# Linear attention on one core: first K and V issued before the tile part closes, programs of three engines moved to aligned blocks and four engines held to the end

## The chip, the cores and the metric

The kernel runs on one core of a Trainium2 chip. The metric is the device time of one execution in microseconds (us). Before the change it is 124.9 us, the median of three runs (124.57 to 125.02).

## The reference

Q, K and V are float32 of shape 8 x 12 x 512 x 64 (batch, heads, sequence, dimension), from a normal draw. With `Qf = max(0, Q)` and `Kf = max(0, K)`, each of the 96 heads computes

- `KV = Kf^T V` (64 x 64) and `Ksum = sum over the sequence of Kf` (64),
- `out = (Qf KV) / (Qf Ksum + 1e-10)`, float32.

There is no softmax, so each of Q, K and V is read once and the output is written once: 37.75 MB read and 12.58 MB written.

## The kernel before, in words

The 96 heads are cut into 12 octets of 8 heads. One octet of one tensor is 128 partitions by 2048 elements, 1 MB of float32. Everything is written for one octet and repeated 12 times. No scheduler takes part: the five engines have programs written out by hand and meet at semaphores.

- GpSimd (POOL) issues nearly all loads (`load`, L109). They cast float32 to bf16 on the way into a ring of six slots each for K, V and Q. Only Q of octet 0 (L96) goes to a slot of its own. POOL also issues the stores of octets 0 to 9 (`store`, L117). Before a load it waits until the ring slot is free again, and before a store until the octet is normed. The order is fixed: eleven rounds of K, V, Q, with stores from the eighth round on.
- SyncE (SP) issues K of octet 0 (L94) as float32 into the output buffer `o_sb[0]`, the stores of octets 10 and 11 (L117), then waits for all twelve stores (L318) and clears the kernel's semaphores (L321).
- ScalarE (ACT) issues V of octet 0 (L95) into `o_sb[1]`. Then per octet it applies relu to the transposed Q out of PSUM (L214), moves the K^T V sums out of PSUM (L219), scales a part of the next V (L208) and copies the products (L228).
- VectorE (DVE) first fills masks, zeros and an identity (L275 to L298). Then per octet: `prep` (relu and mask of K at L237, mask of V at L241), `stage` (a copy of Q, L247), `norm` (the product with the reciprocal, L259) and `denominators` (L262 to L273).
- TensorE (PE) runs `turn` in a hardware loop of 12 rounds (L189): transposes of Q (L158), K^T V (L167), the transposes back of the octet before (`back`, L148), denominators (L176), Q KV (L184). After the loop `back` runs once more. The head of the loop is at the start of an instruction block (`head_slot`).

What stands at the beginning: line 15 closes the tile framework's context at once, before any instruction of the kernel. The closing puts two rounds of an all-engine barrier behind the launch's own barrier (the profile gives them lines 16 and 334). Only behind them come L94, L95 and L96. PE waits at L188 until DVE has finished its masks (`ID` at 4); the first transposes wait for `STG` in any case, which DVE raises after that.

What stands at the end: POOL, ACT, PE and DVE run out of their programs one after the other while SP still waits for the stores.

Octets are stored from nine output buffers in turn (`NOUT`); `norm` waits for the store of nine octets before (L253).

## Time and profile before

| | us |
|---|---|
| median of three runs | 124.9 (124.57 to 125.02) |
| profiled execution, device time | 124.66 |
| its span, from the first to the last instruction | 123.4 |
| POOL busy | 27.5 (22%) |
| DVE busy | 89.3 (72%) |
| PE busy | 87.4 (71%) |
| ACT busy | 79.4 (64%) |
| HBM traffic over the span | 408 GB/s (37.75 MB read, 12.58 MB written) |

How to read it: the span counts from the first instruction that the profiler shows, and all positions below count from there. The 1.3 us between span and device time lie outside it. A load that casts moves 1 MB out of HBM and 0.5 MB into the core's memory; the GB/s of the profile count the half, so 213 GB/s in a stretch of such loads are 426 GB/s read. The chain of work that ended last is 34% DMA and 27% "issue", which is here POOL waiting for ring slots.

The trace also lists each DMA packet (queue, start, length, bytes) and each landing: a transfer of 1 MB is spread over 16 DMA engines, and each of them raises the transfer's semaphore by one when its part is in place. So for each transfer there are 16 landings. Instruction blocks that an engine fetches are packets too, on queues of their own ("instruction" in the profile): 16,384 bytes on one such queue, 8,192 on the other.

### The profile page before, as it was taken

What the parts mean: (1) busy time and instruction counts of PE and PEld (TensorE: products, weight loads), DVE (VectorE), ACT (ScalarE), POOL (GpSimd) and SP (SyncE); (2) the same over time, 40 slices, a digit from 0 to 9 for tenths busy, and PEclk for the clock granted to TensorE, in tenths of its full rate; (3) what the DMA queues carried; (4) which work ended last, traced back from release to release, by engine and by line L of the source; (5) the groups of instructions that cost most, each with busy time, mean ns of one, the idle gap of its engine ahead of it and who ended that gap; (6) DMA issues with size and microseconds to landing.
All of it is one profiled execution on the core that took longest, in us unless ns stands there. A gap on an engine that the chain in (4) does not pass through costs nothing.

```text
span 123.4 us, 3380 instructions
## 1 busy us (share of the span) xinstructions
PE 87.4 (71%) x1456; PEld 75.9 (62%) x1456; DVE 89.3 (72%) x178; ACT 79.4 (64%) x109; POOL 27.5 (22%) x50
## 2 busy tenths in 40 slices
PE   0000099998998979799897998979449939977400
PEld 0000099986886868688686877958429928947200
DVE  3737906599989899998989989897395497091600
ACT  0043063999988888898888889888539649542000
POOL 3999500050240804309101001010010001000000
PEclk9999999999999999999999999999985995996775
DMA  3999999999999999999999999999999999999994
GB/s 43 369 344 217 213 213 213 213 215 213 214 213 213 213 215 213 214 214 217 214 213 214 213 214 221 371 217 214 375 222 214 343 425 428 425 422 433 420 425 170
DMA packets 6918, 32.57 MB, mean 264 GB/s; under 512 B 768, under 2 KB 768, under 8 KB 5120
## 3 DMA queue, kind: packets, MB, share of 16 engines
q0 software_dynamic: 6336, 28.31, 92.2%
q1 hardware_dynamic: 432, 3.15, 6.6%
q10 hardware_dynamic: 144, 1.05, 2.2%
q8 instruction: 2, 0.03, 0.1%
q14 instruction: 4, 0.03, 0.1%
HBM read 37.75 MB, written 12.58 MB: 408 GB/s over the span
## 4 chain that ended last, share of the span: by engine, by line
DMA 34%; issue 27%; POOL 18%; PE 8%; DVE 5%; ACT 1%; POOLq 0%; DVEq 0%
DMA q_all<-in_Q_dram 34%; POOL k_all L109 6%; POOL q_all L109 5%; POOL v_all L109 5%; DVE o_sb L259 5%; PE ps_o L148 4%; PE ps_kv L167 2%; PE ps_q L158 1%; PE ps_o L184 1%; POOL out_dram L117 1%; ACT ot L228 1%; POOL q_all L96 1%; POOL ident L121 0%; POOL ident L119 0%; POOLq L107 0%
## 5 line engine op out<-in xcount | busy, mean ns | idle before, releaser
L259 DVE TENSOR_TENSOR o_sb<-ps_o,rec 128x1024 f32<-128x1024 f32 x24 | 28.3, 1219 | 7.0 <-PE ps_o L148 6.7
L228 ACT COPY ot<-ps_o 128x1024 f32<-128x1024 f32 x24 | 24.2, 1013 | 10.3 <-PE ps_o L184 9.2
L167 PE MATMUL ps_kv<-vo,kf 64*128 64x132 bf16 x768 | 28.6, 230 | 0.7
L148 PE MATMUL ps_o<-ident,ot 128*128 128x128 f32 x208 | 27.1, 286 | 1.1 <-ACT ot L228 1.1
L167 PEld LDWEIGHTS ps_kv<-vo,kf 64*128 64x128 bf16 x768 | 24.8, 100 | 3.8 <-DVE vo L241 2.3
L214 ACT ACTIVATE qt_sb<-ps_q 128x1024 bf16<-128x1024 bf16 x24 | 23.4, 1030 | 5.1 <-PE ps_q L158 5.1
L158 PE MATMUL ps_q<-ident,q_sb 128*128 128x128 bf16 x192 | 15.3, 243 | 15.4 <-DVE q_sb L247 15.4
L148 PEld LDWEIGHTS ps_o<-ident,ot 128*128 128x128 f32 x208 | 23.8, 146 | 2.7 <-ACT ot L228 1.4
L158 PEld LDWEIGHTS ps_q<-ident,q_sb 128*128 128x128 bf16 x192 | 13.2, 110 | 16.7 <-DVE q_sb L247 15.4
L219 ACT CAST kvd<-ps_kv 64x260 bf16<-64x260 f32 x48 | 18.0, 375 | 7.8 <-PE ps_kv L167 7.4
L184 PE MATMUL ps_o<-qt_sb,kvd 128*128 128x256 bf16 x96 | 15.0, 282 | 10.8 <-DVE o_sb L259 9.8
L237 DVE TENSOR_SCALAR kf<-k_all,mask_k 128x1024 bf16<-128x1024 bf16 x44 | 18.3, 459 | 5.6 <-PE ps_kv L167 5.4
L184 PEld LDWEIGHTS ps_o<-qt_sb,kvd 128*128 128x128 bf16 x96 | 7.7, 100 | 15.6 <-DVE o_sb L259 15.0
L241 DVE TENSOR_SCALAR vo<-v_all,mask_v 128x1024 bf16<-128x1024 bf16 x33 | 15.0, 483 | 0.9 <-DMA v_all<-in_V_dram 0.9
L109 POOL DMA_DIRECT2D k_all<-in_K_dram x11 | 8.4, 763 | 32.1 <-DVE vo L241 32.0
L117 POOL DMA_DIRECT2D out_dram<-o_sb x10 | 5.3, 533 | 40.7 <-DVE o_sb L259 40.7
L208 ACT ACTIVATE vo<-v_all,mask_v 128x1024 bf16<-128x1024 bf16 x11 | 12.7, 1155 | 0.3
L247 DVE COPY q_sb<-q_all 128x2048 bf16<-128x2048 bf16 x12 | 8.3, 694 | 5.7 <-DMA q_all<-in_Q_dram 5.7
L109 POOL DMA_DIRECT2D q_all<-in_Q_dram x11 | 8.9, 811 | 0.0
L109 POOL DMA_DIRECT2D v_all<-in_V_dram x11 | 7.6, 687 | 0.0
L176 PE MATMUL ps_q<-kvd,qt_sb 128*128 128x16 bf16 x192 | 6.9, 180 | 0.0
L176 PEld LDWEIGHTS ps_q<-kvd,qt_sb 128*128 128x128 bf16 x192 | 6.7, 96 | 0.2
(24 smaller groups left out, 27.8 us busy)
## 6 DMA issues: line engine op xcount, KB each, us to landing
out_dram<-o_sb POOLq DMA_DIRECT2D x10, 1024.0 KB, 39.8
q_all<-in_Q_dram POOLq DMA_DIRECT2D x12, 512.0 KB, 36.7
k_all<-in_K_dram POOLq DMA_DIRECT2D x11, 512.0 KB, 33.1
v_all<-in_V_dram POOLq DMA_DIRECT2D x11, 512.0 KB, 34.8
out_dram<-o_sb SPq DMA_DIRECT2D x2, 1024.0 KB, 8.4
o_sb<-in_K_dram SPq DMA_DIRECT2D x1, 1024.0 KB, 8.5
o_sb<-in_V_dram ACTq DMA_DIRECT2D x1, 1024.0 KB, 8.8
```

What stands on the lines that cost most here:

```text
L109: PL.dma_start(out=t[:, to:to + n], in_=X[o:o + n].rearrange("n p f -> p n f"), single_packet=True).then_inc(land(f"{c}{o}"), 16)
L148: t = PE.transpose(ps_o[j][:, P * v:P * v + P], ot[:, 8 * j + v].rearrange("p h c -> p (h c)"), ident32)
L158: t = PE.transpose(dst[:, u], q_sb[:, j * (U // 2) + u], ident)
L167: t = PE.matmul(ps_kv[:, half, 0:2 * (D + 2)].rearrange("p (t d) -> p t d", t=2), kf[g][rows, r].rearrange("p s d -> p (s d)"), vo[g][rows ...
L176: t = PE.matmul(ps_den[:, u], qt_sb[:, u], kvd[:, :, 0:2 * D1:2 * D1 - 1], start=True, stop=True, skip_group_check=True)
L184: t = PE.matmul(ps[:, h], kvd[:, 4 * j + h, 1:2 * D + 1], q[:, :, 4 * j + h, :], start=True, stop=True, skip_group_check=True)
L214: AC.activation(qt_sb[:, j * (U // 2):(j + 1) * (U // 2)], ps_q[j].bitcast(bf16).rearrange("p (u f) -> p u f", u=U // 2), Act.Relu)
L219: t = AC.copy(kvd[64 * c:64 * c + 64, s::2, c * D1:c * D1 + D1].rearrange("p (g t) d -> p g t d", t=2), ps_kv[64 * s:64 * s + 64, :, 0:2 * ...
L228: t = AC.copy(ot[:, :, 4 * j:4 * j + 4], ps_o[j].rearrange("p (h u c) -> p u h c", h=4, u=U))
L237: VE.tensor_scalar(kf[g][:, :, s, :], k_rows(o, g), scalar1=0.0, scalar2=mask_k[:, s:s + 1], op0=Alu.max, op1=Alu.mult)
L241: x = VE.tensor_scalar(vo[g][:, :, t, 2:D + 2], v_rows(o, g), scalar1=mask_v[:, t:t + 1], scalar2=None, op0=Alu.mult)
L259: VE.tensor_tensor(dst[:, rs], ps_o[j].rearrange("p (r d) -> p r d", d=D), rec[o % 2][:, rs].unsqueeze(2).to_broadcast([P, R, D]), op=Alu. ...
```

## The change

K and V of octet 0 are issued inside the tile part, in a critical section, before it is closed, so they stand behind the launch's barrier and ahead of the closing's two. Because the tile part now holds instructions, its closing has semaphores of its own to clear; POOL does that between the two barriers.

POOL, ACT and DVE get an alignment directive after the closing (`at_line`): the next instruction is placed at the next multiple of 128 instruction slots, and a branch skips the padding.

At the end, POOL, PE, ACT and DVE each wait for the stores (`hold`) and raise `FIN`; SP waits for `FIN` at 4 and clears. The twelve store semaphores become three single ones (octets 0 to 2, which `norm` waits for), one shared by octets 3 to 9 (`ALL`) and one shared by octets 10 and 11 (`LAST`). PE's wait for `ID` goes away.

```diff
-    tc.close()
-    tc.compile()
...
+    FETCH = 128
...
-    stored = sems(*[f"st{o}" for o in range(NO)])
+    ALL, LAST, FIN = sems("all", "last", "fin")
+    stored = [sems(f"st{o}")[0] if o + NOUT < NO else ALL if o < NO - 2 else LAST for o in range(NO)]
...
-    SP.dma_start(out=k8.rearrange("p r d -> p (r d)"), in_=Kr[0]).then_inc(land("k0"), 16)
-    AC.dma_start(out=v8.rearrange("p r d -> p (r d)"), in_=Vr[0]).then_inc(land("v0"), 16)
+    def at_line(eng):
+        eng.addr_align(FETCH, offset=0, max_nops=0)
+
+    def hold(eng):
+        eng.wait_ge(ALL, 16 * (NOUT - 2))
+        eng.wait_ge(LAST, 32)
+        eng.sem_inc(FIN, 1)
+
+    with tc.tile_critical(no_gpsimd_drain=True):
+        SP.dma_start(out=k8.rearrange("p r d -> p (r d)"), in_=Kr[0]).then_inc(land("k0"), 16)
+        AC.dma_start(out=v8.rearrange("p r d -> p (r d)"), in_=Vr[0]).then_inc(land("v0"), 16)
+
+    tc.close()
+    tc.compile()
+    for eng in (PL, AC, VE):
+        at_line(eng)
     PL.dma_start(out=q_all[:, RING], in_=Qr[0], single_packet=True).then_inc(land("q0"), 16)
...
     for i in range(done, NO - 2):
         store(PL, i)
+    hold(PL)
     for i in range(NO - 2, NO):
         store(SP, i)
...
-    PE.wait_ge(ID, 4)
     with nc.Fori(1, NO + 1, engines=bass.OrderedEngineSet([PE.engine]), head_slot={PE.engine: 0}) as i:
         turn(i)
     PE.wait_ge(OT, NO + 1)
     back(0)
     back(1)
+    hold(PE)
...
         t.then_inc(OT, 1)
+    hold(AC)
...
     norm(NO - 1)
-    for s in stored:
-        SP.wait_ge(s, 16)
+    hold(VE)
+    SP.wait_ge(FIN, 4)
```

## The prediction

> **What bounds the kernel.** I read the page's slices and DMA queues first, then the beginning by engine, then narrow windows at both ends, then the waits of SP's queue, and last the trace's packets and landings.

> ```profile
> DMA  3999999999999999999999999999999999999994
> ...
> q8 instruction: 2, 0.03, 0.1%
> q14 instruction: 4, 0.03, 0.1%
> ```

> The 16 DMA engines are full from the second slice to the last but one, so no compute engine is the bound: the time is when the transfers start, plus their length, plus what is left when the last one ends. The two queues below move instruction blocks and seem negligible; they are not, as shown further on. The beginning (start, duration, engine and line):

> ```profile
> 1.40 0.38 SPq L94 DMA_DIRECT2D o_sb<-in_K_dram  x1
> 1.40 0.39 ACTq L95 DMA_DIRECT2D o_sb<-in_V_dram  x1
> ...
> 1.93 0.67 POOL L96 DMA_DIRECT2D q_all<-in_Q_dram  x1 [1.48 <-POOLq L16]
> ```

> K and V are issued at 1.40 us. Narrow windows (columns end with DMA share and GB/s):

> ```profile
> 2.00:3.50 1.50, 0.00 (x0) 0.00 (x0) 1.12 (x2) 0.00 (x0) 1.10 (x4) 1.00 0.88 137
> 3.50:8.00 4.50, 0.00 (x0) 0.00 (x0) 2.81 (x19) 0.70 (x1) 4.50 (x9) 1.00 0.97 381
> ...
> 120.00:121.00 1.00, 0.00 (x0) 0.00 (x0) 0.00 (x0) 0.00 (x0) 0.00 (x0) 0.50 0.99 418
> 121.00:121.50 0.50, 0.00 (x0) 0.00 (x0) 0.00 (x0) 0.00 (x0) 0.00 (x0) 0.50 0.59 246
> 121.50:122.00 0.50, 0.00 (x0) 0.00 (x0) 0.00 (x0) 0.00 (x0) 0.00 (x0) 0.50 0.20 82
> 122.00:122.50 0.50, 0.00 (x0) 0.00 (x0) 0.00 (x0) 0.00 (x0) 0.00 (x0) 0.50 0.20 82
> ```

> The transfers ramp up for 1.5 us and then run full. At the end most of the 16 engines are done by 121.5, but a share of 0.20, three engines of 16, goes on to 122.5. The waits of SP's queue (total us, times, longest) hold the two barriers' price:

> ```profile
> SPq L334 <- PEq L334: 0.7, 1, 0.7
> SPq L16 <- PEq L16: 0.5, 2, 0.3
> ```

> SP leaves the launch's barrier at 0.66 and the closing's second at 1.32.

> **The stragglers at the end.** In the trace's landings, the last store's 16 parts have their median at 121.76, but four come 0.91, 0.93, 1.28 and 1.37 later, and SP's final wait ends with the latest. The packets say why. Six instruction blocks were fetched while data flowed: 16,384 bytes at 11.50 (took 0.94) and 114.34 (0.97), 8,192 at 32.75, 49.66, 97.46 and 105.55 (0.31 each). From the first one on, one landing of sixteen is late by 1.2 in every transfer, where the three before had at most 0.21. A fetch runs on one DMA engine, and since the queues never empty, that engine never catches up. Whose blocks these are I infer from the instruction counts. The 16 KB ones are PE's: it enters its loop at 7.78 and leaves it at 110.36, with its program running into the next block some 12 slots later. The fetch follows such an entry by 3.7 (7.78 to 11.50). DVE executes 123 instructions between 32.75 and 97.46, about one block, so those are its two. The one at 105.55 comes 3.2 after POOL's last issue ends (102.31): POOL runs on past its program. 49.66 is ACT's.

> **The change part by part.**

> *K and V earlier.* Behind the launch's barrier (SP free at 0.68) stand now a no-operation, a wait for its own count and the issue. The rows between SP's instructions in the barriers are 0.06 apart, so the issue comes at 0.86 to 0.92, ACT's about the same. Against 1.40 that is 0.48 to 0.54. The ramp (first packet 1.01 after the issue) moves with it. Since everything behind it is a full queue, each later transfer moves by it too: **-0.5**. Bounds: 0 (if the ramp waits for something else) and -0.74 (the whole of 0.66 to 1.40).

> *The closing later.* SP and ACT must finish their issues (0.38, 0.39) and report before the closing's first barrier: 0.9 + 0.39, four steps of 0.06 and a barrier of 0.33 put its release at about 1.76. POOL's clearing stands between the barriers (SP's own at the end lasts 0.145 and is the nearest row; I take 0.1 with its drain), then the second barrier at 0.33: POOL is free at 2.15 where it was at 1.29, **0.85 later**, and so are DVE, ACT and PE. Is that covered? DVE's fills end at 7.22 and it then waits 2.75 for K; moved to 8.1 they still end before or at K's landing. ACT's table load (7.30 to 8.58) moves to 9.5 and V is not there before 8. PE starts at 15.4 on DVE's copy. For these three the cost is 0, or up to 0.3 of compute that the full queue hides anyway.

> *POOL's own issue* is the one that can hurt. Q of octet 0 is issued at 1.93 to 2.59, and its first packet runs at 6.31. Until then DMA lives on K and V alone: 16 packets per engine, the first two within 1.45 (2.41 to 3.86), 14 more at 0.306, so alone they last until 2.41 + 1.45 + 4.28 = 8.14, with the change 7.6. Q's first packet moves to 6.31 + 0.85 = 7.16. Margin 0.45: cost 0. POOL's many issues at 0.53 each stay far ahead of DMA (a load lands 33 to 37 after its issue).

> *The alignment.* Three branches over padding, and a new block each. The nearest rows are PE's jump into its aligned loop, 7.35 to 7.78, so at most 0.43 per engine, and a gap of 0.06 between plain instructions. I take 0.1: with POOL at 7.26, still inside the margin. In return ACT's program (about 111 instructions behind the directive) and POOL's (about 55) lie in one block of 128, so the fetches at 49.66 and 105.55 go, and DVE's two become one, near 68. The blocks behind are now asked for at 2.2, while K and V flow, at 0.31 each on their engines. PE enters its loop at about 2.7 instead of 7.78, so its first 16 KB also fall into K's and V's time: the engine is late by 1.0 from there on, as before from 11.5.

> *PE's last fetch*, at 114.34, is the one that decides. The loop is 244 slots (120 products of two instructions each, and four more) of a block of 256, so the 32 slots behind it cross the block's end exactly as before, whether PE is held afterwards or not. I expect the 16 KB again, hence a part 1.1 to 1.3 late. Of the 1.37 now, 0.1 to 0.26 was there before (the landings before 114 show it) and may go: **-0.1**, bounds +0.3 (another early block on the same DMA engine) and -1.2 (no such fetch).

> *The hold.* Last landing, a wait of 0.02 to 0.05 on four engines, one hop to SP (0.03 from a release to its receiver), the clear: **+0.05**; 0 to +0.15. SP's six waits were in line already, so nothing is won. PE's wait for `ID` covered nothing: its first transposes wait for DVE until 15.4.

> Sum: -0.5 - 0.1 + 0.05 = **-0.55** on the profiled 124.66, that is 124.1. That execution lies 0.24 under the median of the runs, to which I carry the gain: 124.9 - 0.55 = 124.35, said as **124.4**. About 0.5%, 0.62 us, is what a measurement of this kernel can tell from no change, so the forecast ends just inside "no difference".

> [...]

> **Rivals.**

> 1. *The stragglers go.* If PE, held, does not fetch at 114, and its early block falls into the ramp, where DMA moves 137 instead of 381 GB/s and has room, the last landing comes 0.2 to 0.8 behind the median instead of 1.37: 0.6 to 1.2 more, 123.1 to 123.8. For it: early requests meet empty queues. Against: PE's crossing is the same, and the request comes 0.8 after K's first packet.

> 2. *DMA runs dry after K and V* (slower). If POOL finds its new block not yet there, it waits for the fetch: 3.2 to 3.7 by the two rows above. Q's first packet then comes at about 10.7, K and V are out at 7.6, and DMA idles 3.0: -0.5 + 3.0 = +2.5, 127.4. It decides from 0.45 of stall on, and the kernel is slower by over 0.5% from 1.6 on; a partial stall gives 125.5 to 126.5. For it: POOL's first issue already comes 0.63 after its release, unexplained. Against: the target is the very next block, and DVE, ACT and POOL show no stall at their crossings now.
> [...]

> 3. *Nothing reaches the end.* The start is won, but two early blocks fall on one DMA engine, or PE's last one on an engine already late by 0.31: -0.5 + 0.3 + 0.1, 124.8.

> **Chances.** Forecast 0.55 (own range 124.0 to 124.9; of it 0.19 below 124.28, which is faster by over 0.5%, 0.36 within). Stragglers go 0.15 (faster). DMA dry 0.22 (0.20 slower, 0.02 within). Nothing reaches the end 0.08 (within). Faster 0.34, within 0.46, slower 0.20. The range takes rival 1 nearly whole and the partial stalls: 123.2 to 125.7.

> **What would show it.** K's issue at 0.86 to 0.92 and its first packet at 1.9; POOL's first issue at 2.7 to 2.9; no gap in DMA at 7 to 8; no instruction packet between 10 and 110 but DVE's near 68; one 16 KB packet near 114 and a last landing 1.1 to 1.3 behind its median. I am wrong if that packet is missing, if POOL's first issue comes after 4, or if the time outside the span (1.3) grows because four held engines now end after the stores.

## The result, and the profile after

The changed kernel takes 127.98 us, the median of six runs (127.82 to 129.65), against 124.86 of the kernel before (124.45 to 125.02) on the same chip. The ratio is 1.0288 with a 95% interval of 1.0254 to 1.0322: slower by 3.1 us, where 124.4, just inside a difference of 0.5%, was forecast. The profiled execution took 127.87, its span is 126.17.

The page of the changed kernel, by slices of 3.2 us:

```profile
span 126.2 us, 3391 instructions
...
POOL 0029997023050431707400101010010000000000
...
DMA  4958999999999999999999999999999999999993
GB/s 75 410 192 156 165 212 213 213 213 216 212 213 214 216 212 213 214 213 213 213 214 212 213 213 217 352 238 217 332 260 213 306 426 423 429 431 421 423 434 156
```

POOL does nothing in the first two slices but fill constants, and DMA, which before the change was full from the second slice on, has a hole from the third slice to the fifth (192, 156 and 165 GB/s, where the row shows some 213 for loads that cast). From there on the row reads as before. The beginning, by the changed kernel's timeline (start, duration, engine and line; "idle before" in brackets):

```profile
0.91 0.39 ACTq L105 DMA_DIRECT2D o_sb<-in_V_dram  x1
0.95 0.38 SPq L104 DMA_DIRECT2D o_sb<-in_K_dram  x1
...
8.32 0.67 POOL L111 DMA_DIRECT2D q_all<-in_Q_dram  x1 [7.87 <-issue]
8.98 0.22 POOL L134 MEMSET ident<- 128x128 bf16 x1
```

K and V go out 0.45 and 0.49 earlier, as wanted. But POOL's first issue, Q of octet 0, comes at 8.32 instead of 1.93, with no semaphore that held it ("issue": the engine waited for nothing that the profile shows). The trace has POOL's branch over the padding at 2.36. The same in windows (DMA share and GB/s at the end of the row), one of the kernel before:

```profile
8.00:11.00 3.00, 0.00 (x0) 0.00 (x0) 1.03 (x2) 1.41 (x2) 3.00 (x7) 1.00 1.08 264
```

and three of the changed kernel:

```profile
3.50:8.00 4.50, 0.00 (x0) 0.00 (x0) 3.11 (x16) 0.00 (x0) 0.00 (x0) 1.00 0.96 386
8.00:11.00 3.00, 0.00 (x0) 0.00 (x0) 0.90 (x4) 0.22 (x1) 2.27 (x6) 1.00 0.42 71
11.00:14.00 3.00, 0.00 (x0) 0.00 (x0) 2.96 (x5) 2.21 (x2) 3.00 (x5) 1.00 0.95 173
```

K and V are in place at 8.2 to 8.4 (median of their 16 landings), Q's first packet runs at 9.69, and for three microseconds DMA moves about a quarter of what it moved there before (71 GB/s against 264).

Where the 3.21 us between the two profiled executions are: K of octet 1 lands at 16.45 against 13.56, **2.89** later, although K and V of octet 0 began 0.48 earlier. From then on the shift stays: Q of octet 11 lands 2.82 later (medians 99.98 and 97.16), the span is 2.81 longer. The other **0.4** lies outside the span, 1.70 against 1.30. The tail did not change: the last landing comes 1.33 behind its median, before 1.37.

### The profile page after: what moved, and what is told of

Read it like the earlier page. It is cut to its first block, busy times and chain, and to the rows that moved or that the text cites. A ratio compares the mean times of both kernels' runs of the same rounds, so it can differ in the third digit from the quotient of the medians.

```text
span 126.2 us, 3391 instructions
## 1 busy us (share of the span) xinstructions
PE 86.5 (69%) x1456; PEld 75.3 (60%) x1456; DVE 89.1 (71%) x178; ACT 79.4 (63%) x109; POOL 28.2 (22%) x50
## 4 chain that ended last, share of the span: by engine, by line
DMA 33%; issue 27%; POOL 18%; PE 6%; DVE 6%; ACT 1%; POOLq 0%; DVEq 0%
DMA q_all<-in_Q_dram 33%; POOL q_all L124 6%; POOL k_all L124 6%; DVE o_sb L277 6%; POOL v_all L124 5%; PE ps_kv L183 2%; PE ps_o L164 2%; PE ps_q L174 1%; PE ps_o L200 1%; POOL out_dram L132 1%; ACT ot L244 1%; POOL q_all L111 1%; POOL ident L136 0%; POOL ident L134 0%; DVEq L276 0%
## 5 line engine op out<-in xcount | busy, mean ns | idle before, releaser
L183 PE MATMUL ps_kv<-vo,kf 64*128 64x132 bf16 x768 | 29.7, 235 | 0.7
L183 PEld LDWEIGHTS ps_kv<-vo,kf 64*128 64x128 bf16 x768 | 25.9, 103 | 3.8 <-DVE vo L259 2.3
L164 PE MATMUL ps_o<-ident,ot 128*128 128x128 f32 x208 | 25.8, 278 | 1.1 <-ACT ot L244 1.1
L164 PEld LDWEIGHTS ps_o<-ident,ot 128*128 128x128 f32 x208 | 22.7, 142 | 2.8 <-ACT ot L244 1.4
L124 POOL DMA_DIRECT2D k_all<-in_K_dram x11 | 7.3, 663 | 27.3 <-DVE vo L259 27.1
L124 POOL DMA_DIRECT2D q_all<-in_Q_dram x11 | 8.4, 765 | 0.0
```

The source lines that it names most:

```text
L124: PL.dma_start(out=t[:, to:to + n], in_=X[o:o + n].rearrange("n p f -> p n f"), single_packet=True).then_inc(land(f"{c}{o}"), 16)
L164: t = PE.transpose(ps_o[j][:, P * v:P * v + P], ot[:, 8 * j + v].rearrange("p h c -> p (h c)"), ident32)
L183: t = PE.matmul(ps_kv[:, half, 0:2 * (D + 2)].rearrange("p (t d) -> p t d", t=2), kf[g][rows, r].rearrange("p s d -> p (s d)"), vo[g][rows ...
```

## Experiments

All were run beside the kernel before; ratios are to its runs on the same chip. "Early K and V alone" is the changed kernel without the alignment of POOL, ACT and DVE, without the hold (SP waits for `ALL` and `LAST` itself; the shared store semaphores stay), and with PE's first wait back.

### First question: is it POOL's alignment, the early K and V, or the hold?

Run `e1_pool_no_line`, the changed kernel without POOL's alignment:

```diff
-    for eng in (PL, AC, VE):
+    for eng in (AC, VE):
         at_line(eng)
```

> The changed kernel with no alignment of POOL's program; ACT, DVE, the early K and V and the hold stay. Theory A (POOL's branch goes to an instruction block that is not there, and its fetch waits behind K's and V's packets): POOL's first issue comes at 2.8 to 3.0 us instead of 8.32, DMA has no gap between 8 and 11, and the time falls by 3.3 to 124.3 - 124.8. Theory B (POOL's first issue is held up by K's and V's transfers under way, wherever its program lies): POOL's first issue stays near 8.3 and the time near 127.9.

124.82 us, ratio 1.0012 (1.0000 to 1.0024). POOL's first issue is at 2.93:

```profile
2.93 0.67 POOL L111 DMA_DIRECT2D q_all<-in_Q_dram  x1 [2.48 <-POOLq L108]
```

The loss comes from POOL's alignment alone, and theory B falls. ACT and DVE stay aligned, and two 8 KB packets still run, at 6.05 and 6.39: POOL does not wait for those.

Run `e2_kv_behind`, K and V issued behind the closing, the rest as changed:

```diff
-    with tc.tile_critical(no_gpsimd_drain=True):
-        SP.dma_start(out=k8.rearrange("p r d -> p (r d)"), in_=Kr[0]).then_inc(land("k0"), 16)
-        AC.dma_start(out=v8.rearrange("p r d -> p (r d)"), in_=Vr[0]).then_inc(land("v0"), 16)
-
     tc.close()
     tc.compile()
+    SP.dma_start(out=k8.rearrange("p r d -> p (r d)"), in_=Kr[0]).then_inc(land("k0"), 16)
+    AC.dma_start(out=v8.rearrange("p r d -> p (r d)"), in_=Vr[0]).then_inc(land("v0"), 16)
     for eng in (PL, AC, VE):
```

> The changed kernel with K and V issued behind the closing, as before the change; alignment of three engines and hold stay. Theory A with a fetch that waits behind data: here POOL branches at 1.4, just as K and V are issued and 1.0 ahead of their first packet, so its fetch meets empty queues; POOL's first issue at 3 to 4, time 124.9 to 125.5. Theory A with a fetch that takes long in any case: POOL's first issue again 5.9 behind its branch, at 7.3, time 127.4 to 127.9. Theory B: as before the change, POOL's first issue at 1.9 to 2.1, time 124.8 to 125.3 with the hold.

125.17 us, ratio 1.0055 (1.0016 to 1.0093). POOL branches at 1.35 and issues at 4.85:

```profile
4.85 0.67 POOL L109 DMA_DIRECT2D q_all<-in_Q_dram  x1 [4.40 <-issue]
```

That is 3.5 behind the branch instead of 6.0. The three 8 KB packets start at 2.42 (together with K's first packets), 4.44 and 6.08. The last one comes behind POOL's issue, so if POOL waits for its own, that is one of the first two; the trace does not say which. In the changed kernel all three come at 6.05 to 6.13, 3.7 behind POOL's branch. My reading is that the two halves of the change hurt each other: with K and V issued ahead of the branch (0.95 and 0.91 against 2.36), POOL's fetch stands behind their packets.

Run `e3_no_hold`, the changed kernel without the four holds (SP waits for `ALL` and `LAST` itself):

```diff
-    hold(PL)
...
-    SP.wait_ge(FIN, 4)
+    SP.wait_ge(ALL, 16 * (NOUT - 2))
+    SP.wait_ge(LAST, 32)
```

> The changed kernel without the hold: SP waits for the shared store counts itself. If the hold is what raised the time outside the span from 1.30 to 1.70 us, that comes back to 1.30 and the time falls by 0.4 to 127.4 - 127.6; POOL's own run past its end brings an 8 KB fetch back near 107. If the 0.4 has another cause, the time stays at 127.9 and the share outside at 1.7.

127.7 us, ratio 1.0248 (1.0209 to 1.0287). 1.31 us lie outside the span: the 0.4 is the hold's. The packet that I expected back near 107 did not come; my reading, which nothing else tests, is that POOL starts in a new block here and has room in it.

Run `e4_kv_only`, early K and V alone:

> Only K and V early and the shared store counts: no alignment, no hold, PE's first wait back. Theory A: the start is won and nothing lost, K's issue at 0.95, first transfers 0.45 earlier, POOL's first issue at 2.9 without a gap in DMA; 124.3 to 124.6. Theory B: POOL's first issue at 8 and 127.4 to 127.6.

124.22 us, ratio 0.9947 (0.9926 to 0.9968): **faster than both kernels**, and than the one before by the 0.5 us that the early issue was to bring. Its beginning, by its timeline and its windows:

```profile
2.93 0.67 POOL L109 DMA_DIRECT2D q_all<-in_Q_dram  x1 [2.48 <-POOLq L108]
3.60 0.22 POOL L132 MEMSET ident<- 128x128 bf16 x1
```

```profile
8.00:11.00 3.00, 0.00 (x0) 0.00 (x0) 1.82 (x5) 2.44 (x2) 3.00 (x7) 1.00 1.09 234
11.00:14.00 3.00, 0.00 (x0) 0.00 (x0) 3.00 (x5) 0.00 (x0) 3.00 (x6) 1.00 1.06 214
```

POOL's first issue is 1.0 later than in the kernel before (forecast 0.85), and DMA has no hole: 234 GB/s where the changed kernel has 71.

### Second question: why does the alignment stall POOL?

Run `e5_pool_line`, early K and V, and POOL's alignment as the only one:

```diff
+    at_line(PL)
     PL.dma_start(out=q_all[:, RING], in_=Qr[0], single_packet=True).then_inc(land("q0"), 16)
```

> Early K and V and the alignment of POOL alone (no hold, no alignment of ACT and DVE, PE's first wait kept). The stall of POOL alone should give back the whole loss: POOL's first issue at 7.5 to 8.4 us, a gap in DMA from 8 on, 127.2 to 127.7. Theory A1 (the block that POOL branches to is not there): before POOL's first issue exactly one or two 8 KB packets, the first of them what POOL waits for, its issue 1 to 2 behind that packet's end. Theory A2 (the block is there, the branch costs in another way): POOL's issue is not tied to the 8 KB packet's end.

126.96 us, ratio 1.0177 (1.0151 to 1.0204), a little under the expected 127.2; the profiled execution took 127.63. One 8 KB packet runs before POOL's first issue, at 6.09 to 6.40. The issue comes 1.41 behind its end:

```profile
7.81 0.67 POOL L110 DMA_DIRECT2D q_all<-in_Q_dram  x1 [7.36 <-issue]
```

That looked like A1, a block that is not there.

Run `e6_pool_nops`, the same, but walking through the padding:

```diff
-        eng.addr_align(FETCH, offset=0, max_nops=0)
+        eng.addr_align(FETCH, offset=0, max_nops=255)
```

> As the run with POOL's alignment alone, but POOL walks through the padding (no-operations) instead of branching over it. Theory A1, in the form that the block is not there however POOL comes to it: the stall stays, first issue at 7 to 8.5, time 127 to 128. Theory A2, in the form that it is the branch which breaks the fetching ahead: no stall, POOL's first issue at 2.93 plus some 60 no-operations at 0.03 to 0.06 (4.7 to 6.5), time 124.2 to 125.2.

129.12 us, ratio 1.0365 (1.0313 to 1.0418), above the expected 128. POOL walks 52 no-operations until 4.41, and its first issue is later still:

```profile
9.35 0.67 POOL L110 DMA_DIRECT2D q_all<-in_Q_dram  x1 [8.90 <-issue]
```

It comes again 1.41 behind the end of the one 8 KB packet (7.94), so it is not the branch. Nor is it the end of K's and V's transfers: their last packets end at 8.16 in the run before and at 8.01 here, while the issue moved by 1.54 together with the fetch.

Run `e8_pool_line_later`, POOL's alignment behind its second round of loads:

```diff
         load(o, n)
+        if o == 2:
+            at_line(PL)
         o += n
```

> Early K and V, and POOL's alignment put behind the first two rounds of its loads instead of ahead of its first issue. Theory A: the branch at about 8 us stalls POOL again for 3 to 6, but two rounds of loads (14 us of transfers) lie queued, so DMA has no gap and the time is that of early K and V alone, 124.0 to 124.4. If a stalled POOL costs in another way than by letting DMA run dry, 126 to 127.

124.28 us, ratio 0.9969 (0.9953 to 0.9985): the time that theory A gave, but not for its reason, since there is no stall at all. POOL branches at 6.61; its timeline:

```profile
6.10 0.56 POOL L122 DMA_DIRECT2D k_all<-in_K_dram  x1
6.62 0.57 POOL L122 DMA_DIRECT2D v_all<-in_V_dram  x1
7.14 0.57 POOL L122 DMA_DIRECT2D q_all<-in_Q_dram  x1
7.66 0.58 POOL L122 DMA_DIRECT2D k_all<-in_K_dram  x1
```

The issues go on at 0.52, and the 8 KB packet comes only at 10.25. No packet before that brought a block, so the block that POOL branches to had been there all along, and **theory A1 falls**: I read the packet as the block behind, fetched ahead. That leaves theory C, for the next two runs: what stalls is POOL's first issue, which waits for a pending fetch as a later one does not. (A "software-made" transfer in the expectations is one that POOL issues, on the queue that the profile calls `software_dynamic`; K and V of octet 0 go over `hardware_dynamic` ones.)

Run `e9_line_behind_q0`, the alignment directly behind POOL's first issue:

```diff
     PL.dma_start(out=q_all[:, RING], in_=Qr[0], single_packet=True).then_inc(land("q0"), 16)
+    at_line(PL)
```

> Early K and V, POOL's alignment directly behind its first issue (Q of octet 0) instead of ahead of it. Theory C (what is held up is the first software-made transfer alone: it can't be issued while POOL's own fetch of the next block is under way): POOL's fetch again runs near 7 us, but the second issue (K of octet 1) comes at 4.5 to 4.7 without a stall; 124.1 to 124.4. Theory D (any issue of POOL is held while a fetch waits behind K's and V's packets in the first microseconds): the second issue comes only at 8 to 9; Q's own packets cover most of that, 124.4 to 125.5.

124.31 us, ratio 0.9956 (0.9932 to 0.9981). Its timeline:

```profile
2.93 0.67 POOL L109 DMA_DIRECT2D q_all<-in_Q_dram  x1 [2.48 <-POOLq L108]
...
4.50 0.56 POOL L123 DMA_DIRECT2D k_all<-in_K_dram  x1 [0.16 <-issue]
5.06 0.54 POOL L123 DMA_DIRECT2D v_all<-in_V_dram  x1
```

The 8 KB packet runs at 6.83, and between the branch and that packet five issues have started without a stall. Theory D falls. One instruction's place is worth 2.6 us (126.96 us with the alignment ahead of the first issue, 124.31 behind it).

Run `e10_fill_first`, the alignment ahead, then POOL's fills, then the first issue:

```diff
+    at_line(PL)
+    PL.memset(ident, 0.0).then_inc(ID, 1)
+    PL.wait_ge(ID, 1)
+    PL.affine_select(out=ident, in_=ident, compare_op=Alu.not_equal, fill=1.0, base=0,
+                     pattern=[[-1, P]], channel_multiplier=1).then_inc(ID, 1)
     PL.dma_start(out=q_all[:, RING], in_=Qr[0], single_packet=True).then_inc(land("q0"), 16)
```

> Early K and V, POOL's alignment ahead, then POOL's fill of the identity (two compute instructions), then the issue of Q. Theory C: POOL's compute instructions run right behind the branch, at 2.5 to 3.2, so the block is there; the issue of Q is still held until 1.4 behind the end of the fetch, at 7.5 to 8; 126.7 to 127.5. If instead POOL's whole program is held for want of its block, the fill too comes only at 6 to 8.

126.84 us, ratio 1.0175 (1.0138 to 1.0213). Its timeline:

```profile
2.84 0.20 POOL L110 MEMSET ident<- 128x128 bf16 x1 [2.40 <-POOLq L108]
3.29 0.28 POOL L112 TENSOR_SCALAR_AFFINE_SELECT ident<-ident 128x128 bf16<-128x128 bf16 x1 [0.24 <-POOL ident L110]
7.96 0.67 POOL L114 DMA_DIRECT2D q_all<-in_Q_dram  x1 [4.39 <-issue]
8.63 0.54 POOL L127 DMA_DIRECT2D k_all<-in_K_dram  x1
```

POOL computes 0.48 behind its branch, so the block was there in this place too. Then it stands for 4.39 us at the first issue, until 1.42 behind the end of its fetch (6.54). Theory C agrees with every run: a first issue with POOL's fetch pending stalls (it comes at 4.85 in `e2_kv_behind` and at 7.81 to 9.35 in the others shown), one without does not (1.93 and 2.93), and neither does a later one (0.52 apart in `e8_pool_line_later`). The 1.4 is not a constant, however. In the changed kernel the issue at 8.32 comes 1.88 behind the last of the three 8 KB packets, and in `e2_kv_behind` at most 1.17 behind POOL's own.

### Third question: the hold, and the tail

Runs `e7_kv_hold` (early K and V with all four holds) and `e12_hold_pool` (with POOL's alone; SP waits for `FIN` at 1):

> Early K and V and the hold, no alignment. If the hold costs 0.35 to 0.4 outside the span, as two profiles with and without it say, the time is 0.3 to 0.5 over the run with early K and V alone (124.22), 124.5 to 124.7, with 1.65 to 1.7 outside the span. If those 0.4 belong to the alignment, it is 124.2 with 1.3 outside.

> Early K and V and the hold of POOL alone. If the 0.4 us outside the span is what each held engine needs to end after the stores, whichever it is, POOL alone already costs it: 1.65 to 1.7 outside, 124.55 to 124.75. If it is another engine's, 1.3 outside and 124.2. No 8 KB packet of POOL's between 100 and 110 in either case.

124.74 us, ratio 1.0002 (0.9983 to 1.0021), 1.69 outside the span of the profiled execution; and 124.77 us, ratio 0.9986 (0.9968 to 1.0003), 1.80 outside. The profiles without a hold have 1.30 to 1.39 outside. POOL's hold alone costs the whole 0.4, and so a hold takes back what the early K and V brought. The 8 KB packet at 105.55 of the kernel before is missing in both, but that is not the hold's doing: these runs have one at 85.07 and 85.31, and so has early K and V alone, without any hold, at 85.22. I take it for the same fetch of POOL's, only earlier, since the runs with POOL aligned ahead of its first issue have none there.

Run `e11_pe_slot128`, early K and V alone with the head of PE's loop in the middle of a block:

```diff
-    with nc.Fori(1, NO + 1, engines=bass.OrderedEngineSet([PE.engine]), head_slot={PE.engine: 0}) as i:
+    with nc.Fori(1, NO + 1, engines=bass.OrderedEngineSet([PE.engine]), head_slot={PE.engine: 128}) as i:
```

> Early K and V alone, with the head of PE's loop at slot 128 instead of 0 of its block, so that the loop crosses a block's end inside and the 32 instructions behind it don't. The prediction's step (PE's fetch near 114 sets the last landing): no 16 KB packet after 100, last landing 1.2 to 1.3 behind its median instead of 1.50 (the next latest engine), 124.0 to 124.1 against 124.2 with early K and V alone. If PE keeps only one block ahead, the loop fetches in every round: ten and more 16 KB packets, 125 to 135.

124.28 us, ratio 0.9942 (0.9920 to 0.9963), no different from early K and V alone and above the expected 124.1. Its DMA queues from 24 to 123 us:

```profile
q0 software_dynamic: 5394, 24.85, 97.6%
q1 hardware_dynamic: 288, 2.10, 5.0%
q14 instruction: 4, 0.03, 0.1%
```

PE's 16 KB queue (q8) is missing: its one packet ran at 22.05, and the loop fetched nothing more. By my estimate it crosses a block's end in each round: it runs 244 instructions from slot 128 on, and a block of 16,384 bytes holds about 250, worked out from the 123 that DVE executes between its two fetches of 8,192 bytes in the kernel before. Yet the last store's latest landings come 1.01, 1.57 and 1.67 behind the median, where early K and V alone has 0.95, 1.25 and 1.50. With PE's last fetch gone, other parts are as late.

## Why the prediction was wrong, point by point

- **K and V earlier: right.** The issues come at 0.91 and 0.95 (forecast 0.86 to 0.92), the first packet is 0.48 earlier (forecast 0.48 to 0.54), and alone this gives a ratio of 0.9947.
- **The closing later: right, though wrongly added.** POOL was released at 2.30 (forecast 2.15), DVE, ACT and PE likewise, and in the run with early K and V alone none of it shows. The forecast's own terms give 1.86 and 2.29, not 1.76 and 2.15; by that the margin was 0.3 and not 0.45. This slip did not make the loss, since early K and V alone has the same late release and no hole.
- **POOL's own issue: this step failed**, as "at most 0.43 per engine, I take 0.1" and "margin 0.45: cost 0". The branch itself costs 0.44 (2.40 to 2.84 in the run with the fill first), about the upper end that was named. What the step left out is a wait. A packet of 8 KB starts 3.7 behind POOL's branch in the changed kernel, as the rows had said of the other fetches; I read it as POOL's fetch of the block behind the new one, standing behind K's and V's packets. POOL's first software-made transfer came only after that fetch had ended, 1.41 and 1.42 beyond it (`e5_pool_line`, `e10_fill_first`) and 1.88 beyond the last of the three packets in the changed kernel. That is 5.4 to 6.0 behind the branch, where 0.1 was put. I had the request at 2.2 in the list and counted only its 0.31 on one DMA engine.
- **Rival 2** had the place (DMA dry after K and V), about the price (+2.5; measured +3.1, of which 0.4 is the hold's) and a chance of 0.22, but the range ended below it. Its mechanism was wrong: the block was there (in `e10_fill_first` POOL fills at 2.84, 0.44 behind the branch). "DVE, ACT and POOL show no stall at their crossings now" was true and no evidence, since none of those crossings stood ahead of POOL's first issue.
- **The alignment's returns: right in place, worth nothing.** The fetches at 49.66 and 105.55 are gone, DVE's two became one (70.33, forecast near 68), and the early ones fell into K's and V's time as forecast: 8 KB three times at 6.05 to 6.13, PE's 16 KB at 6.79. (That the fetch at 105.55 would stay without the alignment was not so: see the third question.) With the hold in both, the run with ACT and DVE aligned (1.0012) and the one without (1.0002) do not differ.
- **PE's last fetch** came (116.88) and the last landing is 1.33 late (forecast 1.1 to 1.3). That it "is the one that decides" was too much: with it gone, the end stays, since other parts are as late (1.67 behind the median in `e11_pe_slot128`, 1.50 in early K and V alone).
- **The hold: mis-sized.** +0.05 forecast with 0.15 as the upper end. Inside the span that is right (0.06 from the last landing to SP's clear), but 0.4 more comes outside the span, which I had named only among what would make the forecast wrong.

What stays open: why the first software-made transfer needs POOL's fetch to be over, and what the time behind it is. The 1.41, 1.41 and 1.42 us are from the three kernels in which POOL fetched alone; in the three in which three engines fetched at once (the changed kernel, `e2_kv_behind`, `e3_no_hold`) the trace does not say which packet was POOL's, and at least in the first two the distance was another. The first issue comes 0.63 behind its release even when nothing is fetched, where later ones follow a wait within 0.02. It also stays open why the kernel ends 0.4 later with POOL held, and whether another engine held alone would cost the same.

## What to carry to other kernels

When a transfer queue is the bound, ask of each step ahead of the first loads what it makes the issuing engine fetch, and what stands in that fetch's way; here, moving other transfers earlier lengthened the way (POOL's first issue came 6.0 behind its branch, against 3.5 in `e2_kv_behind`). Put POOL's first transfer ahead of anything that changes the instruction block: its place, one line further up or down, was worth 2.6 us of 125. A step that took away one late part out of several equally late ones won nothing here (`e11_pe_slot128`, 124.28 against 124.22). Holding POOL to the end had a price of 0.4 outside the profiled span, so compare the device time and not the span alone.
